# PEER layers of an encoder: up products of the last 32 dense tokens from gathered rows, with the up blocks, gates and downs laid out anew

## The chip, the cores and the metric

One core of a Trainium2 chip runs the whole kernel. The metric is the device time of one execution in microseconds. Five engines work side by side, each in order on its own queue: TensorE (PE, with its weight load PEld), VectorE (DVE), ScalarE (ACT), GpSimd (POOL, which issues the indirect transfers here) and SyncE (SP, which issues the other transfers).

## The reference

All data is float32. There are 512 tokens of width 1024 and two layers: layer 0 mixes tokens by neighbourhood attention, layer 1 by a short gated convolution; behind each stands a PEER mixer, which takes most of the time:

```python
q  = (xc @ w_query).reshape(c, 8, 2, 128)
sc = einsum('chpd,hpnd->chpn', q, keys)            # 128 keys per half
sv, si = top_k(sc, 16)
cand = sv[:, :, 0, :, None] + sv[:, :, 1, None, :] # product keys
best, pos = top_k(cand, 16); eidx = ...            # one of 128 x 128 experts
g = softmax(best)
a = einsum('cd,chkd->chk', xc, w_up[eidx])
out = einsum('chk,chkd->cd', gelu(a) * g, w_down[eidx])
```

So every token uses 8 x 16 = 128 of the 16384 experts, and a row of w_up and a row of w_down belong to each.

## The kernel before

The tokens lie in four chunks of 128. Chunk 3 (`c3`) is computed **sparsely**: for each of its 128 picks one indirect transfer on POOL's queue gathers a row of w_up for each token (`gather_up`, a 128x1024 tile `row`), DVE multiplies it with the normed token and sums (`sq`, into a column of `ag`), and one gathers the row of w_down (`gather_down`), which DVE adds to `accg`. The four `row` tiles form a ring, and the gathers come by fours: four ups, then the four downs of the four picks before.

Chunks 0 to 2, 384 tokens (`TD`), are computed **densely**: all 16384 experts, in 128 blocks of 128. One up block (`dense_up`, `up_pieces`, L126/127) is 24 matmuls of 384 columns: eight slices of the width, each with the weights and tokens split into a high and a low part (xh·wh, xl·wh, xh·wl). ACT writes the high part `wu_h` of the weights, DVE the low part `wu_l` (`split`, L105/106), and ACT takes the result through Gelu into `ab` (L510). A down block (`dense_down`) multiplies `ab` by the gates `gt` into `w`, splits `w` and the 128x1024 weights `wd_raw` in the same way, and adds 18 matmuls of 512 columns to six PSUM banks `acc` (L547).

The **gates** are made token by token: a one-hot `oa` over the second key, scaled by the gate values `gT`, times a one-hot `ob` over the first, gives a 128x128 matrix of gates (`ps_gb`, L468). Four tokens make one step; there are 96 steps in a layer. ACT copies each step out of PSUM into `stage` (L469), and every eight steps go to DRAM (`gd`), from where the downs load `gt`, four blocks at a time.

In a layer these stages follow one another: the norm; the queries (`w_query`, blocks of 512 columns) with the top 16 of each half on DVE; the **select stage**, in which `select()` on DVE works out the picks chunk by chunk; the **gate stage**, the 96 steps; and the **down stage**. Up blocks don't need the picks, so the first NPRE = 52 are put into the select and gate stages (PRE_RATE says how many per step), and their `ab` is parked in DRAM (`ad`, back as `at`): the "kept" blocks. The other 76, the "fresh" ones, are computed AHEAD = 4 blocks ahead of their downs. Downs of fresh and kept blocks alternate by fours, and the sparse gathers are spread over the down stage. A scheduler that simulates the engines then fixes the order of the instructions on each engine, so that the order in the program is not the order in the source.

## Time and profile before

| what | us |
|---|---|
| median of 3 runs (3007.44 to 3008.33) | 3007.63 |
| the profiled execution, own time | 3011.78 |
| its span, from first to last instruction | 3010.0 |
| PE busy in the span | 2967.5 |
| DVE busy | 2341.6 |
| ACT busy | 1361.9 |
| POOL busy | 661.2 |

Layer 0 ends at about 1540 us of the span, layer 1 takes the rest. In layer 0 the select stage starts at about 394 us, the gate stage at about 500 us and the down stage at about 720 us. PEclk in the profile is the TensorE clock that was granted, as a share of full speed (2.4 GHz); a profiled execution is somewhat longer than the runs, so sums are made against its own time.

### The profile page before, as it was taken

How to read it: one execution, taken by the hardware profiler on the slowest of the kernel's cores; microseconds unless marked ns; L12 is line 12 of the kernel's file. 1: busy time of each engine (PE TensorE's matmuls, PEld its weight loads, DVE VectorE, ACT ScalarE, POOL GpSimd, SP SyncE). 2: the span in 40 equal slices, each digit the busy share in tenths (PEclk: the TensorE clock that was granted, in tenths of full speed). 3: DMA queues.
4: the chain of work that ended last, by engine and by line, in shares of the span. 5: the costliest groups of instructions: out<-in, count | busy, mean ns of one | idle time of the engine just before them, and what ended most of it. 6: DMA issues, size and time to landing. Idle time of an engine off the chain costs nothing.

```text
span 3010.0 us, 43882 instructions
## 1 busy us (share of the span) xinstructions
PE 2967.5 (99%) x15602; PEld 2657.2 (88%) x15602; DVE 2341.6 (78%) x5115; ACT 1361.9 (45%) x2237; POOL 661.2 (22%) x571
## 2 busy tenths in 40 slices
PE   8999999999999999999999999999999999999998
PEld 6887899999888888888878789999988888888886
DVE  4444999887888887887864489998788878888786
ACT  5454246995333333333332323699733333333333
POOL 0000000002434343443300000000143434444341
PEclk9999999999999999999999999999999999999998
DMA  5222244568999999999933323455799999999994
GB/s 180 91 92 92 93 150 171 218 236 303 340 340 337 342 337 331 346 338 319 322 127 98 112 91 126 165 214 218 265 349 349 332 350 330 340 328 348 328 324 168
DMA packets 297980, 747.94 MB, mean 248 GB/s; under 512 B 23456, under 2 KB 139168, under 8 KB 294688
## 3 DMA queue, kind: packets, MB, share of 16 engines
q1 hardware_dynamic: 224032, 476.67, 45.7%
q0 software_dynamic: 73728, 268.47, 24.3%
q8 instruction: 123, 2.02, 0.3%
q14 instruction: 97, 0.79, 0.1%
HBM read 672.17 MB, written 72.88 MB: 248 GB/s over the span
## 4 chain that ended last, share of the span: by engine, by line
PE 94%; DVE 4%; issue 1%; DMA 1%; ACT 1%; DVEq 0%; ACTq 0%
PE ps_up L127 47%; PE acc L547 35%; PE ps_gb L468 6%; PE ps_o L191 3%; DVE wu_l L106 1%; PE ps_o L298 1%; PE ps_k L409 1%; PE ps_s L261 1%; PE ps_t L175 1%; DMA wd_raw<-in_down 1%; PE ps_pt L285 0%; DVE tk L606 0%; ACT sq L150 0%; PE ps_v L239 0%; DVE best L604 0%
## 5 line engine op out<-in xcount | busy, mean ns | idle before, releaser
L127 PE MATMUL ps_up<-xhf,wu_l 128*128 128x384 f32 (+1 forms) x2304 | 798.4, 347 | 1.1 <-DVE wu_l L106 1.0
L127 PE MATMUL ps_up<-xhf,wu_h 128*128 128x384 f32 (+1 forms) x2304 | 794.3, 345 | 2.6 <-ACT ab L510 2.0
L127 PE MATMUL ps_up<-xlf,wu_h 128*128 128x384 f32 (+1 forms) x2304 | 792.4, 344 | 0.0
L105 ACT ACTIVATE wu_h<-wu_raw 128x1024 fp32r<-128x1024 f32 x336 | 355.4, 1058 | 713.0 <-PE ps_up L127 439.9
L481 POOL DMA_INDIRECT row<-in_up,eidx x256 | 324.2, 1266 | 1276.8 <-DMA wu_raw<-in_up_t 848.1
L547 PE MATMUL acc<-wd_h,w_l 128*128 128x512 f32 x1536 | 602.1, 392 | 0.0
L547 PE MATMUL acc<-wd_l,w_h 128*128 128x512 f32 x1536 | 601.9, 392 | 0.0
L105 ACT ACTIVATE wd_h<-wd_raw 128x1024 fp32r<-128x1024 f32 x256 | 271.5, 1061 | 704.4 <-issue 600.7
L106 DVE TENSOR_TENSOR wu_l<-wu_raw,wu_h 128x1024 fp32r<-128x1024 f32 x336 | 410.4, 1221 | 172.4 <-ACT wu_h L105 170.4
L547 PE MATMUL acc<-wd_h,w_h 128*128 128x512 f32 x1536 | 514.1, 391 | 3.3 <-ACT w_h L105 3.3
L106 DVE TENSOR_TENSOR wd_l<-wd_raw,wd_h 128x1024 fp32r<-128x1024 f32 x256 | 313.4, 1224 | 236.0 <-ACT wd_h L105 228.9
L127 PEld LDWEIGHTS ps_up<-xhf,wu_h 128*128 128x128 f32 x2304 | 433.2, 188 | 21.3 <-ACT ab L510 3.4
L127 PEld LDWEIGHTS ps_up<-xlf,wu_h 128*128 128x128 f32 x2304 | 433.0, 188 | 17.3
L127 PEld LDWEIGHTS ps_up<-xhf,wu_l 128*128 128x128 f32 x2304 | 433.1, 188 | 16.8 <-DVE wu_l L106 3.8
L481 POOL DMA_INDIRECT row<-in_down,eidx x256 | 331.2, 1294 | 512.9 <-DVE sq L488 469.2
L547 PEld LDWEIGHTS acc<-wd_l,w_h 128*128 128x128 f32 x1536 | 288.8, 188 | 59.3
L497 DVE SCALAR_TENSOR_TENSOR accg<-row,ag,accg 128x1024 f32<-128x1024 f32 x256 | 327.7, 1280 | 16.9 <-DMA row<-in_down,eidx 16.2
L547 PEld LDWEIGHTS acc<-wd_h,w_l 128*128 128x128 f32 x1536 | 288.8, 188 | 58.8 <-DVE w_l L106 0.3
L547 PEld LDWEIGHTS acc<-wd_h,w_h 128*128 128x128 f32 x1536 | 287.9, 188 | 57.4 <-ACT w_h L105 4.0
L488 DVE SCALAR_TENSOR_TENSOR sq<-row,hn 128x1024 bf16<-128x1024 f32 x256 | 312.2, 1220 | 3.5 <-DMA row<-in_up,eidx 2.3
L468 PE MATMUL ps_gb<-ob,oa 128*128 128x128 f32 x1536 | 209.4, 274 | 0.0
L469 ACT ACTIVATE stage<-ps_gb 128x512 f32<-128x512 f32 x192 | 204.3, 1113 | 2.1 <-PE ps_gb L468 1.4
(164 smaller groups left out, 3294.3 us busy)
## 6 DMA issues: line engine op xcount, KB each, us to landing
wd_raw<-in_down SPq DMA_DIRECT2D x256, 512.0 KB
wu_raw<-in_up_t SPq DMA_DIRECT2D x256, 512.0 KB
gd<-stage SPq DMA_DIRECT2D x24, 2048.0 KB
gt<-gd SPq DMA_DIRECT2D x64, 768.0 KB
ad<-ab SPq DMA_DIRECT2D x104, 192.0 KB
at<-ad SPq DMA_DIRECT2D x52, 384.0 KB
wu_raw<-in_w_query SPq DMA_DIRECT2D x32, 512.0 KB
wu_raw<-in_w_qkv SPq DMA_DIRECT2D x24, 512.0 KB
```

The lines of the kernel that those rows point to most:

```text
L105: nc.scalar.activation(hi, raw, AF.Copy)
L106: nc.vector.tensor_tensor(lo, raw, hi.bitcast(F32), op=ALU.subtract)
L127: nc.tensor.matmul(ps[:, :n], a[:, c], b[:, kc, :n], start=k == 0, stop=k == 3 * KC - 1)
L175: nc.tensor.transpose(ps[k][:, c * P:(c + 1) * P], hs[c][:, kc * P:(kc + 1) * P], ident)
L191: nc.tensor.matmul(ps[c], a[:, m, c * P:(c + 1) * P], b, start=m == 0 and i == 0, stop=m == KC - 1 and i == 2)
L261: nc.tensor.matmul(ps[hh][:, a * 256:(a + 1) * 256], t["q"][hs, j * P:(j + 1) * P], kk[hs, :, BAND0[j]:BAND0[j] + BAND], start=True, stop= ...
L468: nc.tensor.matmul(ps[:, n * NK:(n + 1) * NK], a, b4[:, n], start=True, stop=True)
L469: nc.scalar.activation(stage[:, :, 4 * q:4 * q + 4].rearrange("p i t -> p t i"), ps.rearrange("p (t i) -> p t i", t=4), AF.Copy)
L481: nc.gpsimd.indirect_dma_start(out=t, out_offset=None, in_=table, in_offset=bass.IndirectOffsetOnAxis(ap=eidx[:, k:k + 1], axis=0))
L488: nc.vector.scalar_tensor_tensor(o, t, 1.0, hn, op0=ALU.mult, op1=ALU.mult, accum_out=ag[:, k:k + 1])
L497: nc.vector.scalar_tensor_tensor(accg, t, ag[:, k:k + 1], accg, op0=ALU.mult, op1=ALU.add)
L547: nc.tensor.matmul(acc[c, half], aa[:, cs], ww[:, hs], start=new and i == 0, stop=n == NK - 1 and ww is held[-1][-1])
```

## The change

The last UT = 32 of the 384 dense tokens (a "unit", the last quarter of chunk 2) leave the dense up blocks: these now have TU = 352 columns. For the unit's 128 picks a token, 32 indirect transfers gather rows of w_up (`urow`, 128 partitions = 32 tokens x 4 picks), DVE multiplies each with the unit's normed tokens `hu` and sums, and ACT and PE bring the results (Gelu, times gate, transposed in `ps_u`) into the unit's columns of `gT`: the one-hot product then puts gate times activation where the other tokens have the gate alone, and `ab` holds 1.0 in those columns. The unit goes through the dense downs as before. `select()` takes chunk 2 first.

Further: NPRE is 72, AHEAD 10; up blocks of the fresh kind are issued behind the last gate product (`issue_after(gb[-1])`); 24 sparse gathers (EARLY) come ahead of the downs; the downs are made in pairs (`w` and its split on 768 columns, `ab` and `at` by pairs), and `gt` is loaded eight blocks at a time. In a gate step one DVE comparison of 128x1024 (`hot`) replaces one of 128x512 (`ob`), one of 128x256 and two of 128x128 (`oa`); ACT scales all four `oa` instead of two; and the copy into `stage` now reads PSUM with a stride of 128 floats and writes runs of four floats, where before it read PSUM in order and wrote single floats 128 bytes apart. In the profile of the changed kernel L134 is the up matmul, L538 the gate product, L537 the scaling, L541 the copy to `stage`, L648 the down matmul, L577 `accg`, L713 and L708 the sums into h.

```diff
-NPRE = 52
-PRE_RATE = 1.4
+NPRE = 72
...
+UN = 1
+UT = 32
+TU = TD - UN * UT
+GB = 8
+PRE_RATE = 1.62
 OB = 12
-ACTN = 2
+
+EARLY = 24
 RING = 4
 RAW = 3
 LAST = 2
-LATE = 0.97
-AHEAD = 4
+LATE = 0.94
+AHEAD = 10
...
+            def unit_lists(gg, ii, jj):
+
+                flat_ids(eid, ii, jj)
+                for u, (q, _) in enumerate(hu):
+                    for g in range(P // UT):
+                        ks = slice(g * UT, (g + 1) * UT)
+                        nc.scalar.activation(fu[ks, u], eid[q, ks], AF.Copy)
+                        nc.scalar.activation(gu[ks, u], gg[q, ks], AF.Copy)
+                nc.vector.tensor_copy(xu, fu)
...
+                        t = wpool.tile([P, D], F32, name="urow", tag="wd_r", bufs=RAW)
+                        nc.gpsimd.indirect_dma_start(
+                            out=t, out_offset=None, in_=up,
+                            in_offset=bass.IndirectOffsetOnAxis(ap=xu[:, u, k:k + 1], axis=0))
+                        urows.append(t)
...
+                        nc.vector.scalar_tensor_tensor(o, urows.pop(0), 1.0, hu[u][1], op0=ALU.mult, op1=ALU.mult,
+                                                       accum_out=au[:, u, k:k + 1])
...
+            def unit_values():
+
+                nc.scalar.activation(au, au, AF.Gelu)
+                nc.vector.tensor_tensor(au, au, gu, op=ALU.mult)
+                ps = ps_acc("ps_u")
+                for u in range(UN):
+                    nc.tensor.transpose(ps[:UT, u * P:(u + 1) * P], au[:, u], ident)
...
-                for c in (3, 0, 1, 2):
+                units = iter(())
+                for c in (cu, c3, 0, 1):
...
-                        b4 = pr.tile([P, 4, NK], F32, name="ob", bufs=OB // 4)
-                        nc.vector.tensor_tensor(b4, iota[:, None, :].to_broadcast([P, 4, NK]),
-                                                iT[:, t:t + 4, None].to_broadcast([P, 4, NK]), op=ALU.is_equal)
-                        a4 = pr.tile([P, 4, NK], F32, name="oa", bufs=OB // 4)
-                        if ACTN:
-                            nc.vector.tensor_tensor(a4[:, :ACTN], iota[:, None, :].to_broadcast([P, ACTN, NK]),
-                                                    jT[:, t:t + ACTN, None].to_broadcast([P, ACTN, NK]),
-                                                    op=ALU.is_equal)
+                        hot = pr.tile([P, 2, 4, NK], F32, name="hot", bufs=OB // 4)
+                        nc.vector.tensor_tensor(hot, iota[:, None, None, :].to_broadcast([P, 2, 4, NK]),
+                                                ijT[:, :, t:t + 4, None].to_broadcast([P, 2, 4, NK]),
+                                                op=ALU.is_equal)
                         for n in range(4):
-                            a, t = a4[:, n], t0 + 4 * q + n
-                            if n < ACTN:
-                                nc.scalar.activation(a, a, AF.Copy, scale=gT[:, t:t + 1])
-                            else:
-                                nc.vector.tensor_scalar(a, iota, jT[:, t:t + 1], gT[:, t:t + 1],
-                                                        op0=ALU.is_equal, op1=ALU.mult)
-                            nc.tensor.matmul(ps[:, n * NK:(n + 1) * NK], a, b4[:, n], start=True, stop=True)
-                        nc.scalar.activation(stage[:, :, 4 * q:4 * q + 4].rearrange("p i t -> p t i"),
-                                             ps.rearrange("p (t i) -> p t i", t=4), AF.Copy)
-                        yield 1.35, 0.9
+                            a = hot[:, 1, n]
+                            nc.scalar.activation(a, a, AF.Copy, scale=gT[:, t + n:t + n + 1])
+                            last = nc.tensor.matmul(ps[:, n * NK:(n + 1) * NK], a, hot[:, 0, n],
+                                                    start=True, stop=True)
+                        gb.append(last.ins)
+                        nc.scalar.activation(stage[:, :, 4 * q:4 * q + 4],
+                                             ps.rearrange("p (t i) -> p i t", t=4), AF.Copy)
+                        yield 1.0, 0.9
...
+            ring = [pp.tile([P, 2, TD], F32, name=f"ab{n}") for n in range(AHEAD // 2 + 1)]
+            for t in ring:
+                nc.gpsimd.memset(t[:, :, TU:], 1.0)
...
             def dense_up(b):
-                for ps in up_pieces(up_t[l, b], xh, xl, TD):
+                for ps in up_pieces(up_t[l, b], xh, xl, TU):
...
+            def load_gates(b):
+                gt = p2.tile([P, TD // GT, GB, GT], F32, name="gt")
...
+                    w = p2.tile([P, 2, TD], F32, name="w", bufs=1)
...
+                    pair.append((mark, *split(w, [P, 2, TD], "w", "w", pool=p2)))
...
-            ng = done = 0
+            ng = EARLY
+            done = 0
...
-                    for _ in ups(nup, top):
+                    with tc.issue_after(gb[-1]):
+                        for i, _ in enumerate(ups(nup, top)):
+                            if i % 4 == 3:
+                                next(early, None)
+                            if n == 0 and i == 4 * KC - 1:
+                                load_gates(b)
+                    nup = max(nup, top)
```

The next rows are PE's order in layer 0, at the end of the gate stage of the kernel before (`ps_up` is an up matmul, `ps_gb` a gate product, x4 are the four tokens of one step):

```order
L468 MATMUL ps_gb<-ob,oa 128x128 x4
L127 MATMUL ps_up<-xhf_2453,wu_l 128x384
L127 MATMUL ps_up<-xhf_2453,wu_h 128x384
L127 MATMUL ps_up<-xlf_2454,wu_h 128x384
L127 MATMUL ps_up<-xhf_2453,wu_l 128x384
L468 MATMUL ps_gb<-ob,oa 128x128 x4
L127 MATMUL ps_up<-xhf_2453,wu_h 128x384
L127 MATMUL ps_up<-xlf_2454,wu_h 128x384
```

There the last step has up matmuls just ahead of it, and up matmuls of the down stage behind it. In the changed kernel the same place reads:

```order
L134 MATMUL ps_up<-xlf_2454,wu_h 128x352
L538 MATMUL ps_gb<-hot 128x128 x3
L134 MATMUL ps_up<-xhf_2453,wu_l 128x352
L538 MATMUL ps_gb<-hot 128x128 x57
L485 MATMUL ps_u<-ident,au 32x128
L538 MATMUL ps_gb<-hot 128x128 x35
L134 MATMUL ps_up<-xhf_2453,wu_h 128x352
L134 MATMUL ps_up<-xlf_2454,wu_h 128x352
```

The last 23 steps (92 products) now stand on PE with no up matmul between them, and 122 up matmuls follow before the first down matmul, where 95 did. Before the first gate product stand 37.1 up blocks (26.0 before), between the first and the last one 34.9 (28.1 before).

ACT's order at that place, in the kernel before (`oa` is the scaling, `stage` the copy out of PSUM, `wu_h` the high part of up weights, `ab` the Gelu of an up block):

```order
L464 ACTIVATE oa<-oa,gT 128x128 x2
L469 ACTIVATE stage<-ps_gb 128x4x128 x2
L464 ACTIVATE oa<-oa,gT 128x128 x4
L469 ACTIVATE stage<-ps_gb 128x4x128
L105 ACTIVATE wu_h<-wu_raw 128x1024
L464 ACTIVATE oa<-oa,gT 128x128 x2
L510 ACTIVATE ab<-ps_up 128x384
```

In the changed kernel:

```order
L541 ACTIVATE stage<-ps_gb 128x128x4 x2
L537 ACTIVATE hot<-hot,gT 128x128 x8
L541 ACTIVATE stage<-ps_gb 128x128x4 x2
L489 ACTIVATE gT<-ps_u 32x32 x4
L541 ACTIVATE stage<-ps_gb 128x128x4
L537 ACTIVATE hot<-hot,gT 128x128 x12
L541 ACTIVATE stage<-ps_gb 128x128x4 x2
```

A step has four scalings and one copy on ACT where it had two and one, and at this place nothing else stands between them.

DVE's order at the end of layer 0 in the kernel before is w_l, w and wd_l of the last downs, the six sums h<-acc and the norm; `accg` and the sum of chunk 3 lie further ahead. In the changed kernel it ends with (`row` is a gathered row, `ag` the factors of chunk 3):

```order
L713 TENSOR_TENSOR h<-acc_8214,h 128x512
L577 SCALAR_TENSOR_TENSOR accg<-row_7740,ag,accg 128x1024
L713 TENSOR_TENSOR h<-acc_8218,h 128x512
L713 TENSOR_TENSOR h<-acc_8222,h 128x512
L713 TENSOR_TENSOR h<-acc_8226,h 128x512
L113 TENSOR_TENSOR wo_l<-wo_raw,wo_h 128x512
L577 SCALAR_TENSOR_TENSOR accg<-row_7741,ag,accg 128x1024
L577 SCALAR_TENSOR_TENSOR accg<-row_7742,ag,accg 128x1024
L577 SCALAR_TENSOR_TENSOR accg<-row_7743,ag,accg 128x1024
L577 SCALAR_TENSOR_TENSOR accg<-row_7740,ag,accg 128x1024
L577 SCALAR_TENSOR_TENSOR accg<-row_7741,ag,accg 128x1024
L577 SCALAR_TENSOR_TENSOR accg<-row_7742,ag,accg 128x1024
```

Eight additions of gathered rows, the last two gather groups, have moved behind the end of the down matmuls; the sum h<-accg of chunk 3 (L708) comes behind the eighth. In layer 1 five of them stand there.

## Rows read from the trace of the kernel before

**Rows 1.** The page: the span, and busy time of each engine.

```profile
span 3010.0 us, 43882 instructions
PE 2967.5 (99%) x15602; PEld 2657.2 (88%) x15602; DVE 2341.6 (78%) x5115; ACT 1361.9 (45%) x2237; POOL 661.2 (22%) x571
```

**Rows 2.** Windows: start:end, length, busy per engine (PE, PEld, DVE, ACT, POOL), clock, DMA share, GB/s.

```profile
386.50:500.50 114.00, 112.46 (x647) 110.25 (x646) 113.02 (x506) 64.88 (x79) 0.00 (x0) 1.00 0.48 159
500.50:703.50 203.00, 203.00 (x1443) 202.96 (x1442) 179.06 (x415) 187.72 (x340) 0.00 (x0) 1.00 0.59 216
722.50:1540.50 818.00, 818.00 (x3972) 723.10 (x3971) 668.42 (x877) 295.03 (x433) 321.74 (x252) 1.00 0.93 332
725.00:775.00 50.00, 50.00 (x240) 43.75 (x240) 42.54 (x61) 19.52 (x29) 18.99 (x16) 1.00 1.01 375
2953.00:2971.00 18.00, 14.72 (x66) 11.88 (x64) 12.52 (x15) 4.54 (x7) 4.94 (x4) 0.97 0.86 314
```

**Rows 3.** The chain that ended last, around the seam (start us, us, what).

```profile
701.06 0.89 PE ps_gb L468 x8
...
703.54 16.47 PE ps_up L127 x95
...
722.45 6.84 PE acc L547 x30
...
736.21 4.18 PE ps_up L127 x24
```

**Rows 4.** Groups by line and shape, PE (busy us, mean ns, idle before).

```profile
L127 PE MATMUL ps_up<-xhf,wu_l 128*128 128x384 f32 x2048 | 698.7, 341 | 1.1 <-DVE wu_l L106 1.0
...
L468 PE MATMUL ps_gb<-ob,oa 128*128 128x128 f32 x1536 | 209.4, 274 | 0.0
```

**Rows 5.** One tile's instructions: one-hots and candidates (count: min/median/max ns, first to last start).

```profile
L454 DVE TENSOR_TENSOR ob<-iota,iT x192: 672/686/715, 470.8 to 2149.4; 128x512 f32<-128x512 f32 x192
...
L614 DVE TENSOR_TENSOR cand<-sv x64: 161/190/330, 394.6 to 1912.3; 128x16 f32<-128x16 f32 x24, 128x64 f32<-128x64 f32 x8, 128x40 f32<-128x40 f32 x8, 128x32 f32<-128x32 f32 x8
```

**Rows 6.** Groups by line and shape, ACT.

```profile
L469 ACT ACTIVATE stage<-ps_gb 128x512 f32<-128x512 f32 x192 | 204.3, 1113 | 2.1 <-PE ps_gb L468 1.4
...
L406 ACT ACTIVATE qpT<-ps_up 128x512 f32<-128x512 f32 x32 | 18.5, 580 | 0.0
```

**Rows 7.** Timeline of ACT in the gate stage (start us, us; records overlap).

```profile
612.91 0.70 ACT L464 ACTIVATE oa<-oa,gT 128x128 f32<-128x128 f32 x2
613.51 1.04 ACT L105 ACTIVATE wu_h<-wu_raw 128x1024 fp32r<-128x1024 f32 x1
614.46 1.08 ACT L469 ACTIVATE stage<-ps_gb 128x512 f32<-128x512 f32 x1
615.33 0.52 ACT L510 ACTIVATE ab<-ps_up 128x384 f32<-128x384 f32 x1
615.76 0.67 ACT L464 ACTIVATE oa<-oa,gT 128x128 f32<-128x128 f32 x2
```

**Rows 8.** Timeline of DVE in the down stage.

```profile
1006.90 1.23 DVE L106 TENSOR_TENSOR wu_l<-wu_raw,wu_h 128x1024 fp32r<-128x1024 f32 x1 [0.93 <-issue]
1008.04 1.22 DVE L488 SCALAR_TENSOR_TENSOR sq<-row,hn 128x1024 bf16<-128x1024 f32 x1
1009.19 0.08 DVE L488 DVE_READ_ACCUMULATOR sq<-row,hn 128x1 f32 x1
```

**Rows 9.** A gather's issue on POOL and its use on DVE, the end of layer 0.

```profile
1504.21 0.94 POOL L481 DMA_INDIRECT row<-in_down,eidx  x1 [1.71 <-DVE accg L497]
...
1511.14 1.29 DVE L497 SCALAR_TENSOR_TENSOR accg<-row,ag,accg 128x1024 f32<-128x1024 f32 x1 [0.32 <-DMA row<-in_down,eidx]
...
1538.26 3.68 DVE L599 TENSOR_TENSOR h<-acc,h 128x512 f32<-128x512 f32 x6 [0.63 <-PE acc L547]
```

**Rows 10.** The chain across the end of layer 0 and at the end of layer 1.

```profile
1529.84 10.67 PE acc L547 x47
...
1544.38 4.33 PE ps_t L175 x18
...
2953.53 15.77 DMA wd_raw<-in_down
...
2996.20 3.68 DVE h L599 x6
...
3003.57 1.19 DVE o L690
```

More of the change, by code (lines that the diff above doesn't have):

```diff
@@ L554, in ups @@
                     yield from dense_up(b)
+            early = early_steps()
+            gb = []
             dve = pe = 0.0
@@ L572, in peer @@
                 order.append(q)
-                while len(kept) and (NPRE // 4 - len(kept)) * len(fresh) <= n * (NPRE // 4):
+                while len(kept) and (NPRE // GB - len(kept)) * len(fresh) <= n * (NPRE // GB):
                     order.append(kept.pop(0))
             order += kept
-            blocks = [4 * q + i for q in order for i in range(4)]
-            ng = done = 0
+            blocks = [GB * q + i for q in order for i in range(GB)]
+            parked = [p2.tile([P, 2, TD], F32, name=f"at{n}", bufs=1) for n in range(2)]
+            for t in parked:
+                nc.gpsimd.memset(t[:, :, TU:], 1.0)
+            ng = EARLY
+            done = 0
             rows = [p2.tile([P, D], F32, name=f"row{n}", bufs=1) for n in range(RING)]
```

157 lines of the change are left out of this document (109 added, 48 removed).

## The prediction

> **What bounds the kernel now.** I read the page first: PE is busy for 2967.5 of 3010.0 us, DVE 78%, ACT 45% [rows 1]. Next the windows by stage, since a share over the span is a mean over different limits [rows 2]. In the gate stage of layer 0 PE is busy 203.00 of 203.00 us, in the down stage 818.00 of 818.00, at a granted clock of 1.00, its level of 2.4 GHz. In the select stage it is busy 112.46 of 114. So every stage is PE's, and the work on PE sets the time. But others are close: in the gate stage ACT has 187.72 of 203 us, in the select stage DVE 113.02 of 114, and in the down stage the DMA share is 0.93 at 332 GB/s, in one stretch of 50 us 1.01 at 375. Shown are stages of layer 0; layer 1 has the same.
>
> Prices on PE come from the chain, where records follow without a gap [rows 3]: 24 up matmuls take 4.18 us, so 174 ns each; 30 down matmuls 6.84 us, so 228 ns; a gate step 0.89 us (four products, each two records, so 1536 over both layers [rows 4]). As a test: the gate stage before holds 96 steps and 28.1 up blocks, 96·0.89 + 28.1·4.18 = 203 us, as measured.
>
> **The narrower up blocks.** A matmul of 512 columns takes 228 ns, of 384 174 ns: 0.42 ns a column. 32 columns fewer are 13.4 ns, 24 matmuls 0.32 us, 256 blocks (2048 records of one of three forms, by eight [rows 4]) **-82 us**, all on the path, since PE is full wherever these blocks stand. An up block then takes 3.86 us. Nothing of down matmuls or gate products is saved.
>
> **Select stage.** Chunk 2's lists and the order of chunks bring a third chunk's selection and 25 of the 32 unit sums ahead of the first one-hot. A unit sum is DVE's sq, 1.14 us to the next record and 0.11 for the read-out [rows 8]: 25·1.25 = 31 us. By DVE's order its work from the first candidate to the first one-hot is about 140 us; before it took 470.8-394.6 = 76 us [rows 5]. PE has 37.1·3.86 = 143 us of up blocks there. Before it had 26.0·4.18 = 109 us for 114 us [rows 2], so some 4 us were lost. The two are as level as before: I take **+2 a layer**, between 0 and 10 (the wait for unit gathers by which DVE could fall behind).
>
> **End of the gate stage.** This is the dear place. The last 23 steps have no up matmul between them, so PE needs 0.89 us a step and ACT sets the pace. ACT starts its records 0.30 us apart for a scaling (613.51-612.91 for two) [rows 7], so four cost 1.20. The copy took 615.33-614.46 = 0.87 to the next start [rows 7]. Its records are 1113 ns long, while a copy of the same 512 elements in order takes 580 [rows 6]; the copy before reads in order, so its excess of about 0.5 us belongs to its write, single floats 128 bytes apart. The new one writes runs of four, and reads with a stride, which no row shows. Its price lies between 0.49 (580 less the overlap of about 0.09 to 0.21 that rows 7 show) and 1.11 (the whole old record). I take 0.49, since rows put the excess on the write alone. A step then costs ACT 1.69, PE waits 1.69-0.89 = 0.80 in each of 23, less some 2.4 us of scalings that a ring of three one-hots lets ACT do ahead: **+16 a layer**. Among the other 73 steps, with 34.9 blocks, PE needs 0.89+0.48·3.86 = 2.74 a step, ACT 1.69+0.48·(0.95+0.43) = 2.35 (wu_h and ab [rows 7]), DVE one comparison of 128x1024 (bounded by wu_l's 1.14 [rows 8]; before 686 ns for half of it [rows 5], and the rest), 0.48 wu_l and 31 sums over 73 steps, 2.2. These are hidden behind PE. Bounds: 0 (if ups fill the place) and 26 (copy at 0.87).
>
> The Trainium skill, "SBUF — State Buffer", section Specifications (TRN2), says that SBUF works in lines of 16 bytes and wants two hits in a line, and PSUM in lines of 8 bytes. The rows agree as to the write; by that rule a read of PSUM at a stride of 512 bytes hits each line once, and the copy may stay at 0.87. No run here shows such a read yet.
>
> **The seam.** Last product, copy, store of `gd`, load of `gt`, w and its split must end before the first down matmul. Before, 95 up matmuls covered it, 16.5 us [rows 3], without a wait. Now 122·0.161 = 19.6 us cover a load twice as large and a w twice as wide. 0.75 MB more at 375 GB/s is 2 us, w and splits about 1.5. The cover grew by 3.1: **+1 a layer** (0 to 4).
>
> **Down stage.** PE has 56·3.86 + 128·4.10 = 741 us, before 74·4.18 + 128·4.10 = 834. Traffic is 56 up blocks, 128 downs and 232 gathers of 0.52 MB, gates 25 and parked pairs 13 MB: 256 MB, 346 GB/s on average. Eight kept blocks in 32.8 us (8 downs, 8·1.34 gathers, gates, pairs: 12.8 MB) want 391, eight fresh ones 333. The rows give 332/0.93 = 357 to 375 GB/s as what the queues carry when full [rows 2]. So a kept stretch lacks 0.5 to 1.1 MB, which the ring buffers of some 3.5 MB cover from the fresh stretches. The last 24 blocks, without ups and with about 1.5 gathers each, want 411 for 98 us: 40 MB against 35 to 37. Beyond the rings up to 1.8 MB are missing, 5 us. Before has such a wait too: 15.77 us of chain on a wd_raw, in a window where PE is busy 14.72 of 18 [rows 2, 10]. **+6 a layer** (0 to 14).
>
> **Ends of the layers.** Before, 1538.26 is the first sum h<-acc, and the transposes of the next layer start at 1544.38, 6.1 us later [rows 9, 10]. Now the eight accg stand there. The first one comes after three sums (0.61 each), three sums, a wo_l and three accg (1.28) more: 9.4 us until the last row is free. Its next gather takes from POOL's issue at 1504.21 to the use at 1511.14, 6.9 us under load [rows 9]; without load I put 4 as a lower bound. Then a last accg 1.28, the sum 1.22 and about 2.4 for the norm: 18.3 to 21.2 instead of 6.1. Chunk 3 stands in every matmul that follows, so it is PE that waits: **+12** in layer 0. In layer 1 five accg remain; the three other chunks' o cover some: **+5**, against sums at 2996.20 and last o at 3003.57 [rows 10]. Bounds 4 and 22 together.
>
> **Moved without a price.** Early gathers and their 24 sums lie under the gate stage on DVE, as counted. The index copies are small ACT work under PE's ups. Pairing leaves the columns of w as they are, with half the starts.
>
> **Sum.** -82 + 2·(2+16+1+6) + 17 = -15 against the profiled execution's 3011.78: 2996.8. The median lies 4.15 below it: **2992**. A change within 0.2%, 6 us either way, can't be told from none here.
>
> **Rivals.** *The copy stays dear.* Strided reading at 0.87 adds 0.38 in the 23 steps, 9 us a layer, and 1 more where ACT passes PE among ups (2.73 to 2.74): 3012, no change. From there ACT sets all 96 steps, and every 0.1 us adds 19 us over both layers: slower by over 0.2% from about 0.88 to 0.9, 3058 at 1.11. For it: no row has a strided read. Against: the old excess sits wholly in the write. Chance 0.2 (0.07 no change, 0.13 slower).
>
> *The transfers bind.* If the queues carry no more than 357 GB/s where gathers and downs meet, and rings don't smooth it since each gather waits for its tile, nine kept stretches of 32.8 us last 35.9, 28 us a layer less the 6 counted: 3036. It decides from a loss of about 16 us a layer. For it: share 0.93 already. Against: 375 held for 50 us with PE full. Chance 0.12 (0.03 no change, 0.09 slower).
> The Trainium skill, "DMA: Bandwidth & Descriptors", section Where 436 GB/s comes from, has about 358 GB/s bind for HBM to SBUF, which would be this rival; the trace's 375 for 50 us is above it.
>
> *Nearly all is hidden.* The narrower ups count whole, ACT's tail shrinks (the waits of the order being shorter on the chip), gathers arrive early at the ends: -82 plus 10 to 45, 2935 to 2972. Chance 0.2.
>
> My forecast, with its own range 2972 to 3001, has 0.48 of the chance, of which 0.04 is no change. Range over the cases: 2946 to 3020. Faster 0.64, same 0.14, slower 0.22.
>
> **What will show it.** The up matmul 161 ns start to start; PE idle some 16 us in the last steps of each gate stage, released by ACT's scaling; the new copy's record near 580 ns or near 1100; the DMA share in kept stretches; accg behind the last down at both ends, with PE idle about 16 us between the layers. I am wrong if the copy is dear, if PE waits on wd or wu weights all through the down stage, or if the tail is filled.

## The result, and the profile after

The changed kernel takes 3047.41 us (median of 4 runs, 3037.13 to 3054.98), the kernel before 3007.53 beside it: 1.0128 times as long, interval 1.0104 to 1.0152. The forecast was 2992 us, faster. The profiled execution is the changed kernel's fastest, 3037.13 us, and the profiled one of before, 3011.78, lies 4 us above its median, so the account below is of 25 us out of 40. The executions of the changed kernel differ by 18 us, those of before by 1.5; what the others lose in addition no profile shows.

The page after, to set against [rows 1]:

```profile
span 3035.3 us, 43253 instructions
PE 2913.4 (96%) x15604; PEld 2598.4 (86%) x15604; DVE 2335.9 (77%) x4410; ACT 1376.2 (45%) x2519; POOL 825.3 (27%) x651
PE 75%; issue 8%; DMA 7%; DVE 5%; ACT 5%; POOL 0%; POOLq 0%; DVEq 0%; ACTq 0%; SPq 0%
```

The chain that ended last is in the third line; before it was

```profile
PE 94%; DVE 4%; issue 1%; DMA 1%; ACT 1%; DVEq 0%; ACTq 0%
```

PE is busy 54 us less, and idle for 122 us instead of 42. The chain runs through PE for 75% only, 94% before; transfers and "issue" (time in which an engine waits for nothing that the profile shows) have 15%. The stages are read from the first and last starts of three tiles: `ps_k`, the key products that end the queries, `ps_gb`, the gate products, and `acc`, the downs. Here those of layer 0:

```profile
L427 PE MATMUL ps_k<-kt,qpT x128: 270/275/276, 301.0 to 395.3; 128*128 128x128 f32 x128
L538 PE MATMUL ps_gb<-hot x768: 270/275/378, 547.9 to 790.2; 128*128 128x128 f32 x192
L648 PE MATMUL acc<-wd_h,w_h x768: 387/389/628, 811.8 to 1537.2; 128*128 128x512 f32 x192
```

The same tiles in both kernels and layers give this table (us). "Idle" is what is left after the work on PE, counted by the order: blocks times 3.86 (4.18 before), steps times 0.89, downs times 4.10. The chain after has 24 up matmuls in 3.86 and in 3.83 us. Of the 37.1 blocks ahead of the first gate product (26.0 before) one stands ahead of the last key product, so 36.1 (25.0) are counted in the second row. The forecast is of what comes on top of before, both layers together.

| stage | before, layer 0 / 1 | after, 0 / 1 | idle after (before), 0 + 1 | forecast |
|---|---|---|---|---|
| start to first key product | 296.8 | 301.0 | 4.2 longer | 0 |
| last key product to first gate product | 108.5 / 108.7 | 152.6 / 155.9 | 13.2 + 16.4 (3.8 + 4.0) | +4 |
| gate stage | 203.5 / 203.5 | 242.3 / 245.8 | 22.0 + 25.6 (0.5 + 0.5) | +32 |
| seam | 16.6 / 16.8 | 21.6 / 20.1 | 2.0 + 0.5 (0 + 0.2) | +2 |
| down stage | 820.2 / 826.4 | 725.9 / 729.0 | 4.6 + 7.7 (3.2 + 9.4) | +12 |
| last down to next key product / end | 208.0 / 12.0 | 229.0 / 23.6 | 21.0 + 11.6 longer | +17 |

With -82 for the narrower blocks the sum is +25, the difference of the spans (3035.3 - 3010.0). The forecast had -15. The 40 us between the two are 18 in the selections, 15 in the gate stages, 16 at the ends of the layers and 4 at the start, less 12 in the down stages.

**Selections.** The windows at the first unit sums (`urow` is a gathered row of the unit, `sq` its sum), with columns as in [rows 2], and the chain through them:

```profile
450.00:460.00 10.00, 9.34 (x59) 9.05 (x58) 7.57 (x13) 4.83 (x7) 4.81 (x4) 1.00 0.76 267
460.00:470.00 10.00, 6.93 (x33) 6.22 (x32) 9.29 (x40) 3.74 (x5) 2.92 (x2) 0.80 0.87 313
470.00:480.00 10.00, 10.00 (x56) 10.00 (x56) 9.82 (x26) 2.82 (x4) 3.56 (x3) 0.86 0.84 272
480.00:490.00 10.00, 10.00 (x64) 10.00 (x64) 10.00 (x39) 5.86 (x8) 2.86 (x3) 1.00 0.89 297
```

```profile
449.63 0.41 POOL urow L468
...
452.00 8.61 DMA urow<-in_up,xu
...
460.71 1.23 DVE sq L475 x2
...
465.93 1.23 DVE wu_l L113
...
467.20 23.70 PE ps_up L134 x131
```

A row is used 11 us after its issue; DVE waits for it, `wu_l` stands behind it on DVE's queue, and PE behind that. PE stands for 3 us between 462 and 467 and then runs at a granted clock of 0.50, its level of 1.2 GHz, before it has 1.00 again:

```profile
464.00:466.00 2.00, 0.24 (x1) 0.24 (x2) 2.00 (x10) 1.71 (x3) 0.03 (x1) 1.00 0.87 301
468.00:470.00 2.00, 2.00 (x8) 2.00 (x7) 2.00 (x4) 0.00 (x0) 0.00 (x0) 0.50 0.89 244
474.00:476.00 2.00, 2.00 (x15) 2.00 (x14) 1.82 (x5) 0.86 (x2) 0.94 (x1) 1.00 0.96 311
```

In the 20 us from 460 on 89 matmuls pass, where the next 10 us alone have 64: at that pace about 6 us are lost for 3 of standing. A short wait is paid twice.

The waits are the smaller part of this stage, though. From the last key product to the first gate product, after and before:

```profile
395.30:547.90 152.60, 145.26 (x877) 142.11 (x876) 147.49 (x531) 78.84 (x104) 32.14 (x28) 0.98 0.76 256
391.30:499.80 108.50, 106.96 (x612) 104.75 (x611) 107.72 (x481) 62.97 (x77) 0.00 (x0) 1.00 0.49 161
```

DVE is busy for 147.5 of 152.6 us and waits for unit rows for 3.7 (7.0 in layer 1), while the up blocks there are 139.4 us of work on PE. So DVE's work sets this stage. It did so before: 107.7 of 108.5 us on DVE, 104.7 of up blocks on PE.

**Gate stage.** The scaling and the new copy (groups by line), then two windows at its end:

```profile
L537 ACT ACTIVATE hot<-hot,gT 128x128 f32<-128x128 f32 x768 | 242.8, 400 | 30.2 <-DVE hot L532 29.8
...
L541 ACT ACTIVATE stage<-ps_gb 128x512 f32<-128x512 f32 x192 | 108.9, 592 | 8.8 <-PE ps_gb L538 5.8 <-DMA gd<-stage 2.6
```

```profile
740.00:760.00 20.00, 18.95 (x138) 18.38 (x137) 15.93 (x14) 19.79 (x55) 0.00 (x0) 1.00 0.67 242
760.00:791.00 31.00, 23.78 (x151) 21.67 (x151) 19.28 (x16) 30.84 (x95) 0.00 (x0) 1.00 0.33 139
```

The copy takes 592 ns, near the 580 that the forecast took, where [rows 6] had 1113. In the last window ACT is busy 30.84 of 31 us; 145 records of gate products at 0.111 and five up matmuls are 17 us of work on PE, so 14 us are idle. Counted over all 23 steps that stand alone, from the last up matmul to the last gate product, 37.5 us pass for 20.5 of work: this is the forecast tail, 17.0 us idle in either layer where 16 were forecast, at 1.63 us a step. The other 5.0 and 8.6 us lie earlier, where DVE waits for the rows of the early gathers (`erow`) for 7.0 and 8.2 us.

**Ends.** The chain between the layers, and the windows there:

```profile
1536.06 0.70 DVE h L713
...
1543.08 1.11 POOL row L558
...
1545.24 5.33 DMA row<-in_down,eidx
...
1553.30 1.24 DVE h L708
...
1559.12 5.58 PE ps_t L183 x24
```

```profile
1537.00:1545.00 8.00, 1.06 (x5) 0.56 (x3) 7.93 (x11) 1.29 (x3) 3.72 (x3) 0.77 0.81 268
1545.00:1553.00 8.00, 0.00 (x0) 0.00 (x0) 5.32 (x5) 0.00 (x0) 2.04 (x2) 0.50 0.57 197
1553.00:1562.00 9.00, 2.88 (x13) 2.55 (x14) 6.22 (x26) 4.95 (x12) 0.20 (x4) 0.50 0.00 0
```

From the first sum to the transposes (`ps_t`) pass 23.1 us, where [rows 9, 10] have 6.1. PE stands for 21.1 us and comes back at a granted clock of 0.50. The other 4 of the 21 us come behind the transposes, about as much as at the start of layer 0.

### The profile page after: what moved, and what is told of

Read it like the earlier page. It is cut to its first block, busy times and chain, and to the rows that moved or that the text cites. A ratio compares the mean times of both kernels' runs of the same rounds, so it can differ in the third digit from the quotient of the medians.

```text
span 3035.3 us, 43253 instructions
## 1 busy us (share of the span) xinstructions
PE 2913.4 (96%) x15604; PEld 2598.4 (86%) x15604; DVE 2335.9 (77%) x4410; ACT 1376.2 (45%) x2519; POOL 825.3 (27%) x651
## 4 chain that ended last, share of the span: by engine, by line
PE 75%; issue 8%; DMA 7%; DVE 5%; ACT 5%; POOL 0%; POOLq 0%; DVEq 0%; ACTq 0%; SPq 0%
PE ps_up L134 33%; PE acc L648 33%; PE ps_gb L538 3%; PE ps_o L199 3%; ACT hot L537 2%; DMA urow<-in_up,xu 2%; DMA wd_raw<-in_down 2%; DVE wu_l L113 1%; DMA erow<-in_up,eidx 1%; ACT stage L541 1%; DMA erow<-in_down,eidx 1%; PE ps_o L306 1%; DMA gd<-stage 1%; PE ps_s L269 1%; ACT sq L157 1%
## 5 line engine op out<-in xcount | busy, mean ns | idle before, releaser
L134 PE MATMUL ps_up<-xhf,wu_h 128*128 128x352 f32 (+1 forms) x2304 | 773.5, 336 | 12.1 <-ACT ab L602 8.5
L134 PE MATMUL ps_up<-xhf,wu_l 128*128 128x352 f32 (+1 forms) x2304 | 774.9, 337 | 8.8 <-DVE wu_l L113 8.7
L134 PE MATMUL ps_up<-xlf,wu_h 128*128 128x352 f32 (+1 forms) x2304 | 770.8, 335 | 0.0
L648 PE MATMUL acc<-wd_h,w_h 128*128 128x512 f32 x1536 | 600.2, 392 | 11.7 <-ACT wd_h L112 9.8
L648 PE MATMUL acc<-wd_h,w_l 128*128 128x512 f32 x1536 | 600.5, 391 | 0.0
L648 PE MATMUL acc<-wd_l,w_h 128*128 128x512 f32 x1536 | 491.0, 390 | 0.0
L134 PEld LDWEIGHTS ps_up<-xhf,wu_h 128*128 128x128 f32 x2304 | 437.5, 190 | 31.0 <-ACT ab L602 10.9
L134 PEld LDWEIGHTS ps_up<-xhf,wu_l 128*128 128x128 f32 x2304 | 437.3, 190 | 26.0 <-DVE wu_l L113 12.9
L134 PEld LDWEIGHTS ps_up<-xlf,wu_h 128*128 128x128 f32 x2304 | 437.7, 190 | 13.9
L648 PEld LDWEIGHTS acc<-wd_h,w_h 128*128 128x128 f32 x1536 | 289.4, 189 | 68.9 <-ACT wd_h L112 11.5
L648 PEld LDWEIGHTS acc<-wd_l,w_h 128*128 128x128 f32 x1536 | 288.1, 188 | 59.4
L648 PEld LDWEIGHTS acc<-wd_h,w_l 128*128 128x128 f32 x1536 | 289.8, 189 | 54.6
L577 DVE SCALAR_TENSOR_TENSOR accg<-row,ag,accg 128x1024 f32<-128x1024 f32 x240 | 307.4, 1281 | 13.4 <-DMA row<-in_down,eidx 12.1
L567 DVE SCALAR_TENSOR_TENSOR sq<-row,hn 128x1024 bf16<-128x1024 f32 x224 | 273.4, 1220 | 7.5 <-DMA row<-in_up,eidx 6.1
L532 DVE TENSOR_TENSOR hot<-iota,ijT 128x1024 f32<-128x1024 f32 x192 | 231.0, 1222 | 58.7 <-PE ps_gb L538 58.5
L537 ACT ACTIVATE hot<-hot,gT 128x128 f32<-128x128 f32 x768 | 242.8, 400 | 30.2 <-DVE hot L532 29.8
```

Source lines behind the costliest of these rows:

```text
L134: nc.tensor.matmul(ps[:, :n], a[:, c], b[:, kc, :n], start=k == 0, stop=k == 3 * KC - 1)
L532: nc.vector.tensor_tensor(hot, iota[:, None, None, :].to_broadcast([P, 2, 4, NK]), ijT[:, :, t:t + 4, None].to_broadcast([P, 2, 4, NK]), o ...
L537: nc.scalar.activation(a, a, AF.Copy, scale=gT[:, t + n:t + n + 1])
L567: nc.vector.scalar_tensor_tensor(o, t, 1.0, hn, op0=ALU.mult, op1=ALU.mult, accum_out=ag[:, k:k + 1])
L577: return lambda: nc.vector.scalar_tensor_tensor(accg, t, ag[:, k:k + 1], accg, op0=ALU.mult, op1=ALU.add)
L648: nc.tensor.matmul(acc[c, half], aa[:, cs], ww[:, hs], start=new and i == 0, stop=n == NK - 1 and ww is held[-1][-1])
```

## The experiments

My theory after the result: the narrower blocks pay in full, and the gain is lost where gathered rows and their sums share queues with what feeds PE. The rivals: transfers bind everywhere; ACT's fourth scaling or DVE's sums set the gate stage; other parts of the change cost by themselves. Times are medians, for orientation 3007 before and 3047 changed; stages are read as above, and the work in them is counted by each run's own order.

**The narrowing alone.**

```diff
-                for ps in up_pieces(up_t[l, b], xh, xl, TD):
+                for ps in up_pieces(up_t[l, b], xh, xl, TD - 32):
...
```

> The kernel before with one part of the change: its dense up blocks have 352 columns, and 1.0 stands in the last 32 columns of each block's activations; the up products of those 32 tokens are left out, with nothing in their place. If the narrower blocks pay in full wherever they stand, 256 blocks at 0.32 us take 82 us away: 2925 us, up to 2940 with the few gathered rows that the order here leaves behind the last down at each layer's end. If instead transfers, DVE or ACT can't feed a PE that is 8% faster in the gate and down stages (the rival for why the changed kernel is slow), the time stays above 2970, with PE idle spread over the down stage.

2970.48, 0.9878 times before [0.9862, 0.9895]. By the number that is the edge of what the rival expects, by the place it is neither: the down stages are 788.6 and 788.7 for 787.3 of work, so the price of a block holds and nothing starves there. But only 37 of the 82 us are left in the time, without a single row gathered for the unit: so the theory's "in full" does not hold. Among the selections 11 us a layer are idle, 7 more than before: the stretch takes 110.8 us, 2 longer than before, for 99.9 of up blocks, with DVE busy for 107.9. Further 8 and 9 are lost in the seam, where this order leaves 2 up blocks as cover instead of 4, and 13 and 7 at the ends.

**Up matmuls between the last gate steps.**

```diff
+                    with tc.issue_after(gb[-1]) if gb else ExitStack():
+                        if next(pre, 0) is not None:
+                            break
```

> The changed kernel, with each piece of an up block that is planned behind a gate step held behind that step's last product on PE, so that up matmuls stand between the last 23 steps as well. My theory: in the changed kernel the gate stage takes 242 and 246 us where its work on PE is 220, since ACT's five instructions a step (1.69 us) pace the steps that stand alone. Then the gate stage shows no more than 6 us of idle PE, and the time falls by about 35 us, to some 3010; another 10 may come from the layer ends, where this order leaves three or one gathered rows behind the sums instead of eight and five. The rival, that waits for gathers or the clock set the gate stage's time wherever the ups stand, expects less than 10 us from the gate stage.

3076.04: slower. The gate stage takes 232.7 for 202 of work, so 31 are still idle. Its windows in the last third:

```profile
685.00:705.00 20.00, 19.26 (x136) 18.41 (x135) 15.49 (x14) 20.00 (x58) 0.00 (x0) 1.00 0.49 183
705.00:725.00 20.00, 18.50 (x135) 17.84 (x134) 14.89 (x13) 20.00 (x58) 0.00 (x0) 1.00 0.65 256
```

ACT is full: it has no time for the high parts and Gelus of more blocks, so moving matmuls there fills nothing. DVE is full in the first 40 us. The blocks pushed behind the stage lengthen the seam to 45.7, of which 12 are idle. (In e5 below, without the unit's sums, the same scalings and copies leave PE idle for 2.6 and 4.0 us in this stage.)

**Five row tiles.**

```diff
-RING = 4
+RING = 5
```

> The changed kernel with five tiles for gathered rows in the down stage instead of four; by its order all additions of gathered rows then stand ahead of the last downs. My theory: chunk 3's sum, waiting for two round trips of gathers behind the last downs, costs some 15 us and a slow start of the clock at the end of layer 0 and 11 at the end of layer 1. Then the first transposes of layer 1 start 6 to 7 us behind the last down instead of 21, the kernel ends some 12 us behind the last down instead of 23.6, and the time falls by about 27 us, to some 3020. The rival: the gathers are late because the transfers are slow, so that DVE waits for them in the down stage instead, PE waits for DVE, and less than 10 us is gained.

3058.6. The ends shrink as expected (213.5 and 12.8), the down stages grow by 22 and 24 us. A hundred us of the blocks without up matmuls, in this run and in the changed kernel:

```profile
1418.00:1518.00 100.00, 89.14 (x362) 72.17 (x361) 80.99 (x94) 29.39 (x35) 50.59 (x35) 0.91 0.93 333
```

```profile
1412.00:1512.00 100.00, 96.72 (x418) 79.26 (x417) 85.61 (x100) 33.21 (x38) 47.81 (x31) 0.98 0.96 344
```

The rival is right as to the transfers: in these blocks they carry 333 to 344 GB/s, and the granted clock falls to 0.91. PE waits for ACT's `wd_h` (35.7 us in the run), with a `wd_raw` of 17.8 us in the chain, and not for DVE as the rival had it. Nearly all that the down stages lose lies behind the last up matmul, here and in the changed kernel. I read it so: rows that arrive in time take the place of `wd_raw`, and the rows behind the last down were the same shortage, paid elsewhere. This run alone does not show it, since its order also leaves 41 and 39 downs behind the last up matmul instead of 35.

**Unit sums behind the first one-hots.**

```diff
+                        with tc.issue_after(hots[-1]):
+                            nc.vector.scalar_tensor_tensor(o, urows.pop(0), 1.0, hu[u][1], op0=ALU.mult, op1=ALU.mult,
+                                                           accum_out=au[:, u, k:k + 1])
```

> The changed kernel with the sums of the unit's gathered rows held on DVE behind the first one-hots, so that none of them stands among the selections; 8 of the up blocks ahead of the first gate product move behind it with that. My theory: in the selections DVE stands waiting for gathers that land 8 to 9 us after their issue, the low parts of up weights queue behind it, PE stands idle and then runs for some us at a lower granted clock: 9 and 12 us a layer. Then PE loses no more than 3 us there, and the time falls by about 18 us, to some 3029. The rival: the wait goes with the sums, since the transfers are crowded in the gate stage as well (DMA share 0.85 to 0.97), and PE loses the same in the gate stage: less than 6 us is gained.

3022.29, 25 less. The stretch to the first gate product is 110.3 and 110.4 us, with 108.6 of up blocks and DVE busy for 110.1: of 13 and 16 us idle 2 are left. The sums have taken both their work on DVE and their waits along, so this run does not part the two; the rows of DVE above do. The gate stages (276.9, 273.0, with 251 of work) lose 26 and 22, as in the changed kernel.

**All but the unit.**

```diff
-UN = 1
+UN = 0
```

> The changed kernel without its unit: up blocks of 384 columns again, no rows of w_up gathered for dense tokens, all else as changed (72 blocks ahead, ten up blocks behind the last product, 24 early gathers, pairs, one comparison a step, four scalings on ACT, the new copy). Work on PE is that of the kernel before. By its order up matmuls stand between the gate steps to the end and all gathered rows ahead of the last downs. My theory, that what the unit gains is lost where it crowds DVE and ACT among the gate steps and the transfers behind them, expects no change against the kernel before, 3000 to 3015. The rival, that one of the other parts costs by itself (ACT's fourth scaling, gates by eight blocks, downs in pairs), expects over 3025.

3067.55: the rival. What came with the unit costs 60 us without it, and the unit itself gives 20 back. The seams take 55.5 and 58.9 for 46 of work, the down stages 754 for 742, and the stretches to the first gate product lose 3 and 7 more than before. The seam in layer 0:

```profile
763.00:773.00 10.00, 10.00 (x60) 10.00 (x59) 3.28 (x3) 2.88 (x4) 4.89 (x4) 1.00 1.04 359
773.00:783.00 10.00, 5.29 (x31) 4.97 (x29) 0.00 (x0) 0.98 (x2) 0.00 (x0) 0.89 1.05 389
783.00:793.00 10.00, 7.60 (x28) 7.10 (x29) 2.45 (x2) 2.67 (x3) 0.00 (x0) 0.60 0.66 230
```

The transfers are full there. On SyncE's queue the next up weights stand behind the last store of gates, two loads of gates of 1.5 MB each and the first two loads of parked pairs (`at`). The issue of these two holds SP for 9.7 us, and for 4.4 in the kernel before:

```profile
763.91 9.73 SPq L623 DMA_DIRECT2D at<-ad  x2
713.98 4.39 SPq L527 DMA_DIRECT2D at<-ad  x2
```

Half of all issues of such a load take under 0.4 us in e5, under 0.7 before. SP issues no weights meanwhile; why it takes so long no run shows.

**On the kernel with late unit sums (e4)**, next: the unit's copies later (e6), and on that 40 early gathers (e7) or the fourth scaling on DVE (e8).

```diff
+                if hp == 7:
+                    for u in range(UN):
...
-EARLY = 24
+EARLY = 40
...
+                            if n < 3:
+                                nc.scalar.activation(a, a, AF.Copy, scale=gT[:, t + n:t + n + 1])
+                            else:
+                                nc.vector.tensor_scalar(a, a, gT[:, t + n:t + n + 1], None, op0=ALU.mult)
```

> The kernel with the unit's sums behind the first one-hots (the run before), and the unit's normed tokens, with their three copies on ACT, made after the eighth query block instead of in the norm. My theory: in the changed kernel the three copies of 1.05 us stand on ACT ahead of the first high parts of the normed tokens, and the first query products come 4.2 us late in layer 0 and as much in layer 1. Then the first key product of layer 0 starts at 297 us instead of 300 to 301, and the time falls by 8 us against the run before it (3022), to 3014. The rival: these copies are hidden or only move, less than 3 us.

3024.56, no change; the multiplication still stood in the norm, so this tells nothing.

> The same with 40 instead of 24 sparse gathers taken ahead of the downs; by its order nothing of chunk 3 stands behind the last downs. My theory after the run with five rows: in the last 24 blocks, which have no up block, a PE that needs a block of weights every 4.1 us and 1.5 gathered rows with it wants 411 GB/s and the transfers carry 340 to 350; the rows come late there or behind the end. With 16 gathers, 8 MB, fewer in each down stage both go: the ends shrink by 15 and 11 us, the down stages stay at 725 to 732 us, and the time falls by about 25, to some 2990. The rival: the gate stage, in which DVE is then busy with 16 more sums of 1.25 us, grows by as much as is gained, 3010 to 3030.

3014.65, 10 less than e6. The ends give 16 and 12, the down stages are 720.0 and 719.7 with 6 idle, the gate stages stay (278.6, 278.3), but the seams grow to 41.3 and 39.5 for 27 of work. The number is the rival's, its reason is not: right as to the ends, and the new wait is the seam's, not the gate stage's.

> The kernel of the run with late sums and late copies, with the fourth of the four scalings of each gate step on DVE instead of ACT. If ACT's 1.69 us a step is what sets the gate stage (my theory for the changed kernel's last 23 steps, and for the steps with up matmuls ahead of them in the run that held ups between the steps), the stage falls by 10 us or more a layer, 20 in all, to some 2994. If DVE, with its sums of gathered rows and low parts, sets it, 27 us more on DVE make it longer, by up to 20 us a layer: over 3020.

3024.86, gate stages 274.6 and 275.7: neither. PE's waits for scalings fall from 18.2 to 8.7 us, and a step that stands alone takes 1.45 and 1.57 us instead of 1.68 and 1.74, so ACT's scalings do pace these steps. But this order leaves 28 and 27 of them instead of 22, and DVE is busy 253 of 275.

**Copies pinned late (e9, on e7); gates by four (e10, on e9); short sums (e11, on e9); a fourth tile (e12, on e10):**

```diff
+                        with tc.issue_after(behind[0]):
+                            nc.vector.scalar_tensor_tensor(t[q], h[q, cu], rs[cu][q], t[q], op0=ALU.mult, op1=ALU.mult)
...
-GB = 8
+GB = 4
...
+                        nc.vector.scalar_tensor_tensor(o[:, 0:64], urows.pop(0)[:, 0:64], 1.0, hu[u][1][:, 0:64], op0=ALU.mult, op1=ALU.mult,
...
-RAW = 3
+RAW = 4
...
-AHEAD = 10
+AHEAD = 4
...
```

> The kernel with forty early gathers, with the unit's normed tokens and their copies now held behind the eighth query block on DVE and ACT; in the two runs before them the program still had the multiplication in the norm (a DVE record of 1.29 us between the scalings of the chunks), so that their expectation of 8 us was not tried. My theory: the first key product of layer 0 then starts at 296 to 297 us, as in the kernel before, instead of 300, layer 1 gains as much, and the time falls from 3014.7 by 7 to 8 us, to about 3007. The rival, that the lateness is the norm's own in its new order of chunks, expects no change.

3011.42, 3 less, within the spread of either run's times. The two places give the 8 us that were expected: 297.8 instead of 300.0 at the first key product, and 209.4 instead of 215.0 from the last down to the second. But the down stages take 7 and 4 more.

> The run before it with gates loaded for four blocks (0.75 MB) instead of eight (1.5 MB), and blocks taken by fours. My theory for the seam, in which PE loses 13 to 14 us a layer in the runs with late sums and 10 to 12 in the one without the unit: up weights stand on SyncE's queue behind the last store of gates (2 MB) and two loads of 1.5 MB, each some 13 us to landing. With half of each load the seam falls from 40 us to under 32, and the time by some 15 us, to 2992. The rival, that the store and the many up blocks behind it fill the seam's transfers anyway, expects less than 5 us.

2987.43, 24 less, but only 7 of it in the seams (37.1, 36.4; in layer 0 the first load of parked pairs still holds SP for 9.0 us, 10.2 in e9), 23 in the down stages (715.0, 713.4), and 6 given back in the gate stages. `GB` sets more than the load: in the changed kernel fresh and kept blocks alternate by eights, here by fours as before. All of the 13 and 10 us that the down stages lost in e9 lay behind the last up matmul, and this order leaves 31 downs there instead of 35. Which of the two it is, the smaller loads or the order of blocks, no run separates.

> The kernel with copies pinned late, but each of the unit's 32 sums takes 64 of the 1024 columns: the same gathers, the same waits for their landing, 37 us less work on DVE in a gate stage; the rest of those products is left out. If DVE's time is what sets the gate stage there (253 of 275 us busy, and up to 20 in waits, in the run with three scalings on ACT), the stage falls from 278 us to 255 to 260, the time by about 40 us. If the waits for landing or ACT's scalings set it, the stage falls by less than 8 us.

2996.61; gate stages 276.7 and 276.9, as with whole sums. The work of these sums on DVE does not set them. The 15 us came from the seams, 31 each: 19 less, of which 8 are the work of a block that this order has in the down stage.

> The run with gates by four, with four instead of three tiles for the unit's and the early rows (and for the weights), each used three gathers later, and four instead of ten up blocks ahead to make room. If DVE's waits for rows that land 8 to 10 us after their issue set the gate stage, it falls from 278 us by 10 to 14 us, and the time by 20 to 28 against the run with gates by four. If DVE's work sets it, the stage stays within 5 us; seam and ends may move by 10 us, since this order leaves some gathered rows behind the last downs in layer 0.

2968.54, **0.9863 times before [0.9847, 0.9879]**, the best here. Gate stages 271.4 and 270.6, seams 29.3 and 35.3. Of the 20 us idle in a gate stage 18 to 19 are now the tail of 21 lone steps.

**Two numbers, a rate, and scalings.** The changed kernel with GB = 4 (e13); then on the best run 48 early gathers (e14), with PRE_RATE = 1.5 (e15), or with the edits of e2 and e8 (e16); and e10 with AHEAD = 4 alone (e17).

> The changed kernel with one number put back: gates loaded, and blocks taken, by four instead of eight. In the runs above that was worth 3.6 us a seam and 10 to 12 us a down stage. If loads of 1.5 MB cost the changed kernel as much, the time falls from 3047 by 15 to 28 us, to 3020 to 3032. If its down stage already gives way by leaving gathered rows behind the last down (its down stages of 726 and 729 us lose only 4 to 8), the gain is under 8 us.

3035.26, 12 less: between the two. The seams are 5.2 and 2.9 shorter, but only because one up block less stands in each; by idle time they go from 2.0 and 0.5 to 0.6 and 1.5. The down stages hold that block, are as long as in the changed kernel, and lose 2.1 and 2.4 instead of 4.6 and 7.7.

> The run with four row tiles ahead, with 48 instead of 40 early gathers; by its order nothing of chunk 3 stands behind the last downs of layer 0 either, where the run before left eight rows. The step from the last down to layer 1's first key product falls from 220 to 209 us; the gate stages may grow by some us with eight more sums of 1.25 us, if they are not hidden. The time: 2968 less 8 to 11, 2958 to 2962. The rival, that gate stage and seam grow by as much: no change.

2983.24, the rival: 10 us come from the end of layer 0, but the order now has 288 and 260 up matmuls in the seam, which takes 63.0 and 55.7 us for 46 and 42 of work.

> The run with 48 early gathers, with up blocks handed out at a rate of 1.5 instead of 1.62; by its order the last steps without an up matmul between them are 10 instead of 21. If ACT's pace in those steps (1.69 us against 0.89 on PE) is the idle time that is left in the gate stage, it falls by 11 times 0.8, about 9 us a layer, and the time by 15 to 18. If ACT has no time left for up blocks either, since scalings, copies, high parts and Gelus fill it in the last third, the gate stage stays within 4 us.

2980.53. The gate stages fall to 263.8 and 262.2, by 8 and 9, as ACT's pace would have it: 9 to 11 idle are left, 8 and 9 of them in the 10 lone steps. Seams with 288 up matmuls in both layers (65.3, 66.3) take it back.

> The run with 48 early gathers, with three scalings a step on ACT and one on DVE, and with up pieces held behind the steps that they are planned for, so that up matmuls stand between all steps to the end. ACT then needs 1.39 us a step and 0.39 blocks of 1.38 us, 1.93; PE 0.89 and 0.39 times 3.86, 2.41: PE should be the bound of every step, and the gate stage, with 37.9 blocks 232 us of work on PE, should show less than 10 us of idle PE, where the other runs show 20 to 26. The time falls by 20 us or more against the run with 48. If it stays, the bound is neither ACT nor the place of the up blocks, but the rows' landing and DVE's queue.

3024.88, gate stages 284.1 and 287.3 for 232 of work. The largest of PE's waits (engine, line, what it waited for, us, times, longest):

```profile
PE ps_gb L545 <- DVE hot L544: 55.7, 46, 4.8
```

With one scaling, 80 sums and the comparison on DVE the bound has changed engines; the expectation had no count of DVE's work.

> The run with gates by four (2987), with four instead of ten up blocks ahead and nothing else: of the two parts of the run with four row tiles (2968.5) the other one. If the fourth tile, with which DVE waits less for rows that have not landed, shortened the gate stages (275.9 and 279.6 to 271.4 and 270.6), they stay here at 275 to 280, and the time between 2983 and 2990, but for the rows that this order leaves behind the last downs of layer 0. If the shorter lead of the up blocks was it, the gate stages fall to 271 and the time to 2970 to 2976.

2982.15, gate stages 275.4 and 274.5. So the fourth tile took most of the 19 us: 4 us in each gate stage, 8 and 2 in the seams; the shorter lead took 5. Ahead of the lone steps DVE waits 7.7 and 12.9 us for unit and early rows here, and 0.5 and 1.7 in e12, so in the gate stage the tile helps by the rows, more than by the weights, which have one more tile as well.

## Why the prediction was wrong

**The narrower up blocks, -82: the price is right, "all on the path" is not.** A block takes 3.83 to 3.86 us, and the down stages are 726 and 729, of which 721 is work. But narrowing alone (e1) leaves 37 of the 82 us. The forecast had PE full wherever these blocks stand. Among the selections it was not: before, DVE was busy for 107.7 of 108.5 us there and the up blocks on PE took 104.7.

**"I take +2 a layer" for the selections: mis-sized, 9.4 and 12.4 more than before.** The bound of 10 named the wait for unit gathers, and I took the low end because works were level (143 us on PE, 140 on DVE). They are not level. The 140 (142 in the trace) run from the first candidate, 8 us behind the last key product, and the 143 from one block ahead of it; counted over the same stretch DVE is busy for 147.5 of 152.6 us and the up blocks take 139.4. DVE's work is the larger part of the loss, and the waits for rows, 3.7 and 7.0 us, come on top: a row 11 us from issue to use in a ring of three stops DVE, then PE, then the clock. Without the sums (e4) 2 us idle are left.

**The end of the gate stage, +16: the tail was right, "hidden behind PE" was not.** The tail took 17.0 us in either layer, and with 10 lone steps instead of 21 (e15) the stages fell by 8 and 9. Another 5.0 and 8.6 us lie among the other steps, which the forecast held to be hidden. A fourth tile took DVE's waits for rows away there, and 4 us a layer with them (e12 against e17), so the rows' landing is part; one cause for the rest isn't shown. PE has 220 us of work, ACT is busy for 213 and DVE for 198 in about 240, and they are full one after the other: in e2 DVE early and ACT late. Less work on one alone, e8 or e11, did not shorten the stage. The rival of a dear copy fell at once (592 ns). The Trainium skill, "SBUF — State Buffer", Specifications (TRN2), by whose 8-byte lines of PSUM a strided read might have stayed dear, is not borne out for ACT's read: 592 ns against 580 in order.

**Down stage, +6, and ends, +17: one shortage, put in the wrong place.** The down stages lost no more than before; the ends lost 33 and the start 4. The forecast named the last 24 blocks that want 411 GB/s, and it counted the round trips at the ends as if they were apart from it. By the order 35 downs stand behind the last up matmul, not 24. From the first sum to the transposes I had 18.3 to 21.2 us and booked the low end, +12; it took 23.1, +17. e3 joins the two: rows in time cost 22 and 24 us of down stage, rows late cost 15 and 11 at the ends. With fewer rows (e7) both ends shrink and the down stages do not grow. Unit copies ahead of the norm's first high parts I had priced at nothing; moving them gives 2.2 us at the start of layer 0 and 5.6 at that of layer 1 (e9).

**The rival "the transfers bind", chance 0.12, held in part**: in the last blocks and in long seams, not in kept stretches as it said. The Trainium skill, "DMA: Bandwidth & Descriptors", section Where 436 GB/s comes from, has about 358 GB/s for a core from HBM. The down stages here carry 333 to 351 over 100 us, near that; over 10 us the seam of e5 has 389.

**Gates and blocks by eight, seen only as 2 us of seam,** cost 24 us in e10 and 12 in the changed kernel (e13). With them all but the unit is 60 us slower than before (e5); how much of the 60 is theirs no run shows. I judged the parts by their work on engines and not by what stands behind them on a queue.

Open: why the changed kernel's executions differ by 18 us, those of e12 by 5; and what holds SP and PE in the long seams.

## What to carry to other kernels

When work is taken off the busiest engine and put on engines that run level with it, ask for each stage which engine is full there, over the same stretch for all of them, and add up waits as well as work: in-order queues pass a late row on, and the bound engine pays again in its clock. Where a term has a range, say why its low end should hold; here it was booked twice and missed twice. Ask of each transfer what is queued behind it. A gain by narrowing here was kept only after late rows, a small ring and the grouping by eights were mended, one by one: 2968.5 instead of 3047.4.

## What the runs showed of the hardware

ACT reads PSUM at a stride of 512 bytes, and writes runs of four floats, at about the price of a copy in order (592 and 580 ns for 128x512), while the copy that writes single floats 128 bytes apart takes 1113 [rows 6]. A PE that has stood for 3 us in all between 462 and 467 runs at a granted clock of 0.50 from 468 to 470 and has 1.00 again at 474; one that has stood for 21 us starts at 0.50. Two issues of parked pairs on SP, right behind two loads of gates, hold its queue for 9.7 us in e5 and 4.4 in the kernel before.
